# Attention over 64 heads: exponentials on VectorE assembled by addition, eight groups instead of six, four pairs transposed by DMA

## The chip, the cores and the metric

The kernel runs on one core of a Trainium2 chip. The metric is device time in microseconds of that core, as the median of several executions; the profile is of one further look at a single execution. Engines in the text: PE (TensorE: matrix products and transposes), ACT (ScalarE: exponentials), DVE (VectorE), POOL (GpSimd), SP (SyncE, which issues nearly all transfers).

## What is computed

Plain attention for 8 batches of 8 heads, 512 positions, 64 columns, all in fp32:

```python
scale = 1.0 / np.sqrt(q.shape[-1])
scores = np.einsum('bhqd,bhkd->bhqk', q, k) * scale
scores = scores - scores.max(axis=-1, keepdims=True)
attn = np.exp(scores)
attn = attn / attn.sum(axis=-1, keepdims=True)
return np.einsum('bhqk,bhkd->bhqd', attn, v)
```

The kernel leaves out the subtraction of the maximum (the inputs are normal deviates, so the scores are small) and divides at the end.

## The kernel before

**Tiling.** Two heads make a pair `g`, 32 pairs in all. For a pair, SP loads k, q and v (256 KB each, fp32, 128 partitions). POOL casts k and q to fp16 into one tile `qkp` (two casts, `cast_qk`, L334) and v into one of twelve `vp` tiles beside a column of ones (`cast_v`, L329). PE transposes `qkp` in eight 128x128 blocks into a PSUM bank `tp` (`transposes`, L351), and DVE copies the bank to `tqk` in SBUF (`copy`, L359). Scores come out transposed: a block (g, c, h) is 128 keys of chunk c against the 512 queries of head h. Two blocks make a group, one `st` tile of 128x1024 fp32 in PSUM, of which there are three; so PE can be at most three groups ahead of whoever reads them. There are 127 full groups and two halves at the end. An exponential turns `st` into `pt` in fp16 (`scores`, L368), on ACT (L388) or on DVE. A unit of `values` (L462) is four products of 128 queries: the weights are 128x128 pieces of `pt`, one from each chunk, the moving operand is `vp` with its ones column (65 columns). Seven units share a PSUM bank `o`; `normalise` (L446) takes the reciprocal of the ones columns (L449) and multiplies (L450) into a ring of 56 units, from which SP stores one head at a time (L458). `tp` and `o` share two PSUM banks, so a bank is free only when DVE has copied or normalised it.

**The exponential on DVE.** Before, a group takes seven DVE instructions. `raise_` (L399) reads the scores once from PSUM and writes z, the exponent in fixed point, as an integer whose bits are laid out as an fp32 number: this frees `st`. Six passes follow in SBUF (`pass_`, L411): m (mantissa bits with the exponent of 1.0), e (the exponent bits), and four steps of a polynomial, `scalar_tensor_tensor` with two tensor inputs (L437); the last one multiplies by e and writes fp16 into `pt`.

**The order of the work** is written out ahead by a small planner (`Plan`, L17). It steps through an imagined time, holds costs for each kind of step (L31 to L38), and decides what PE and DVE do next. Each engine then runs its list in that order and waits on semaphores where data or buffers are not there. What matters here:
- `for_dve` (L85) gives a group to DVE if the number of passes still to do is at most `AHEAD`, fewer than `MOST` were given, and the pair isn't among the last `LAST_PAIRS`.
- `step_dve` (L199) prefers a raise, then the oldest job that is due; otherwise it starts a pass, but only if every known copy or norm comes due later than the pass's end less `LATE_COPY` or `LATE_NORM`. The pass's end is its cost times `MARGIN`.
- The `values` that need a group from DVE may be planned from its last pass's end plus `SLACK` (L226).
- `step_pe` (L176) prefers scores, holds PE back for them up to `SOON`, and then takes transposes or values.

**Feeding.** `feed(g)` (L346) stands in front of the first scores of pair g. It puts the loads of pair g+5 on SP's queue and the casts of pairs g+3 (k, q) and g+2 (v) on POOL's. SP issues in order, and a load waits until POOL has cast what was in its buffer.

**The start.** `first_pair` (L521) handles pair 0 by hand. While its first loads are under way, PE runs filler products `busy` on constants (L573 to L576): six of 512 columns and two of 128.

Of the kernel before, what the change touches and what calls it, by code (L numbers as in the profile page):

```python
# [8 lines left out]
FP32 = mybir.dt.float32  # L9
# [7 lines left out]
class Plan:  # L17
# [11 lines left out]


    SLOT, EXP, EXP_DONE, EXP_FIXED = 216, 853, 181, 64  # L31
    INTO, OUT_OF = 95, 105
# [4 lines left out]
    NORM_COLUMN, PASS_DONE = 67, 80  # L37
    PASSES = (690, 950, 1335, 1335, 1335, 1250)  # L38
    FIRST_EXP = 5260
    STEP = 5  # L40
    FIRST_UNIT = 4

    LATE_NORM, LATE_COPY, HURRY, SOON, BACKLOG = 200, 200, 900, 220, 1000
    LAST_PAIRS, AHEAD, MARGIN, SLACK, MOST = 2, 0, 1.1, 2000, 6

    def __init__(self, groups, pairs, first):
        self.groups, self.pairs = groups, pairs
        self.pe, self.act, self.dve = 7000, self.FIRST_EXP, 7000
        self.m, self.tiled = first, True
        self.read = []  # L50
        self.exps = {}
        for m in range(first):
            self.act += self.EXP + self.EXP_FIXED
            self.exps[m] = self.act + self.EXP_DONE
            self.read.append(self.exps[m])
        self.tq = {0: 5800}
        self.next_t = 1
        self.part_t = 0
        self.banks = [5100, 5800]
        self.todo = [(g, h) for g in range(pairs) for h in range(2)]  # L60
        self.head = None
        self.units = self.FIRST_UNIT
        self.member = {b: m for m, grp in enumerate(groups) for b in grp}
        self.ready = []
        self.passes = []
        self.on_dve = []
        self.steps = []
# [108 lines left out]
    def step_pe(self, t):  # L176
        if self.m == len(self.groups):
            self.values(t)
            return
        g = self.groups[self.m][0][0]  # L180
        backlog = self.act - t
# [60 lines left out]
def kernel(  # L242
# [28 lines left out]
    cpool = ctx.enter_context(tc.tile_pool(name="const", bufs=1))  # L271
    lpool = ctx.enter_context(tc.tile_pool(name="load", bufs=6))
    qpool = ctx.enter_context(tc.tile_pool(name="qk16", bufs=3))
    tpool = ctx.enter_context(tc.tile_pool(name="tqk", bufs=4))
    ppool = ctx.enter_context(tc.tile_pool(name="pt", bufs=30))
    dpool = ctx.enter_context(tc.tile_pool(name="pd", bufs=3))
    wpool = ctx.enter_context(tc.tile_pool(name="work", bufs=1))
    opool = ctx.enter_context(tc.tile_pool(name="out", bufs=4))
# [4 lines left out]

    HALVED = range(20, 25)
    NU = 56
# [20 lines left out]
    def load_tile(g, name):  # L306
# [4 lines left out]
            name=f"{name}32_{g}",  # L311
            bufs=6,
        )
# [20 lines left out]
    def cast_qk(g):  # L334
# [9 lines left out]
        qkp[g] = t  # L344

    def feed(g):  # L346
        load(g + 5, "kqv")
        cast_qk(g + 3)
        cast_v(g + 2)
# [18 lines left out]
    def scores(m, on_dve):  # L368
        grp = groups[m]
        size = len(grp)  # L370
        st = ps_st.tile([P, 2, S], FP32, tag="st", name=f"st_{m}")
        pool, tag = (dpool, "pd") if on_dve else (ppool, "pt")
        pt = pool.tile([P, 2, S], FP16, tag=tag, name=f"pt_{m}")
        for x, (g, c, h) in enumerate(grp):
# [10 lines left out]
        if on_dve:  # L385
            raised[m] = {"st": st, "pt": pt}
            return
# [7 lines left out]

    QUARTIC = (-0.15702577, 12.31057107, 23.05394928, 37.67975386)
    SHIFT = -6 - 0.20724975786214195

    def raise_(m):  # L399
# [4 lines left out]
            in0=r["st"][:, :, :],  # L404
            scalar1=scale * 1.4426950408889634 * 2.0**23,
            scalar2=(127 + SHIFT) * 2.0**23,
            op0=AluOp.mult,
# [3 lines left out]
    def pass_(m, s):  # L411
        r = raised[m]
        if s == 0:
            r["m"] = wpool.tile([P, 2, S], U32, tag="m", name=f"m_{m}")
            nc.vector.tensor_scalar(  # L415
                out=r["m"][:, :, :],
                in0=r["z"][:, :, :],
                scalar1=0x007FFFFF,
                scalar2=0x3F800000,
                op0=AluOp.bitwise_and,  # L420
                op1=AluOp.bitwise_or,
            )
            return
        if s == 1:
            r["e"] = wpool.tile([P, 2, S], U32, tag="e", name=f"e_{m}")
            nc.vector.tensor_scalar(  # L426
                out=r["e"][:, :, :],
                in0=r["z"][:, :, :],
                scalar1=0xFF800000,
                scalar2=None,  # L430
                op0=AluOp.bitwise_and,
            )
            r["y"] = wpool.tile([P, 2, S], FP32, tag="y", name=f"y_{m}")
            return
        n = s - 2
        mant = r["m"][:, :, :].bitcast(FP32)
        nc.vector.scalar_tensor_tensor(  # L437
            out=r["pt"][:, :, :] if n == 3 else r["y"][:, :, :],
            in0=mant if n == 0 else r["y"][:, :, :],
            scalar=QUARTIC[n],  # L440
            in1=r["e"][:, :, :].bitcast(FP32) if n == 3 else mant,
            op0=AluOp.add,
            op1=AluOp.mult,
        )
# [76 lines left out]
    def first_pair():  # L521
# [50 lines left out]

        for n in range(6):  # L573
            busy(st0[:, 0], S)
        for n in range(2):
# [34 lines left out]
    with tc.manual_schedule():  # L610
        first_loads()
        load(1, "kq")
        load(0, "v")
        for g in range(2, 5):
            load(g, "kq")
            load(g - 1, "v")
        load(4, "v")
        make_identity(nc, ident)
# [50 lines left out]
```

## Time and profile before

Five runs: median 123.02 us, 122.82 to 123.41.

| quantity | value |
|---|---|
| profiled execution, its time | 122.82 us |
| its span (first to last instruction) | 121.0 us |
| exponentials on ACT / on DVE | 118 full groups, 2 halves and 4 of the first pair / 6 |
| DVE busy | 98.9 us, 171 instructions |
| POOL busy | 76.3 us, 93 casts on POOL after the first pair |
| PE products for scores / values / transposes | 248 / 1008 / 248, without the first and last pieces |
| DMA | 33.8 MB, mean 279 GB/s over the span |

How to read it: a group of instructions is named by its line, engine, operation and tiles (written <- read); then come its busy time, the mean duration of one, and the engine's idle time just before it with what ended that. Instructions of one engine can overlap at their ends, so count times mean is more than the busy time. A timeline row is start, length, engine, line, operation, and the idle time before it in brackets.

### The profile page before, as it was taken

To read this page: it belongs to the slowest core of one execution; us is meant where nothing else is said; L and a number is where in the kernel's file an instruction comes from. 1 tells how busy PE (TensorE), PEld (TensorE's weight loads), DVE (VectorE), ACT (ScalarE), POOL (GpSimd) and SP (SyncE) were. 2 spreads that over 40 slices of the span, in tenths; PEclk is the share of its full clock that TensorE was granted. 3 is DMA by queue.
4 is the path that set the end of the run, shared out by engine and by line. 5 is a ranking of instruction groups with operands and counts; after the bars stand their busy time and mean duration, and the time that the engine had idled before them with its cause. 6 is when DMAs were issued, how large, how long until landed. Compare 5 with 4: busy or idle time off the path is not lost.

```text
span 121.0 us, 3953 instructions
## 1 busy us (share of the span) xinstructions
PE 102.9 (85%) x1557; PEld 65.5 (54%) x1557; DVE 98.9 (82%) x171; ACT 114.4 (94%) x127; POOL 76.3 (63%) x101
## 2 busy tenths in 40 slices
PE   7977879879898899878888889987989987898970
PEld 2634455538366567544656646645655754576450
DVE  1549699999996989999999998889997999746261
ACT  4699999999999999999999999999999999999970
POOL 2368999997687968868595886268965539100000
PEclk9999999999999999999999999999999999999999
DMA  4999999997999999999969998999997994033253
GB/s 123 281 365 384 384 378 384 376 301 250 286 304 366 380 339 289 298 374 355 350 204 248 330 350 281 252 333 335 344 336 252 293 328 144 0 121 102 93 167 96
DMA packets 35604, 33.82 MB, mean 279 GB/s; under 512 B 2689, under 2 KB 35585, under 8 KB 35585
## 3 DMA queue, kind: packets, MB, share of 16 engines
q1 hardware_dynamic: 35152, 33.24, 84.6%
q10 hardware_dynamic: 432, 0.33, 0.8%
q8 instruction: 12, 0.20, 0.6%
q14 instruction: 8, 0.06, 0.2%
HBM read 25.17 MB, written 8.39 MB: 277 GB/s over the span
## 4 chain that ended last, share of the span: by engine, by line
ACT 45%; issue 19%; PE 12%; DVE 10%; DMA 4%; SPq 3%; POOL 2%; ACTq 0%; POOLq 0%
ACT pt L388 45%; PE st L383 6%; DMA q<-in_q_dram 4%; PE o L471 4%; DVE y L437 3%; SPq L327 3%; DVE tqk L364 2%; DVE ring L450 2%; PE tp L357 2%; POOL qkp L340 2%; DVE pt L437 1%; SPq L515 1%; POOL vp L332 1%; DVE rc L449 0%; DVE obl L499 0%
## 5 line engine op out<-in xcount | busy, mean ns | idle before, releaser
L388 ACT ACTIVATE pt<-st 128x1024 f16<-128x1024 f32 (+1 forms) x120 | 109.5, 1273 | 0.2
L383 PE MATMUL st<-tqk 64*128 64x512 f16 x248 | 45.5, 382 | 9.8 <-ACT pt L388 7.6
L471 PE MATMUL o<-vp,pt 128*128 128x65 f16 x1008 | 41.8, 194 | 0.7 <-POOL vp L332 0.5
L471 PEld LDWEIGHTS <-pt 128*128 128x128 f16 x1008 | 35.8, 98 | 11.8 <-issue 11.4
L340 POOL CAST qkp<-k 128x512 f16<-128x512 f32 x31 | 24.7, 795 | 21.8 <-DMA k<-in_k_dram 13.1
L332 POOL CAST vp<-v 128x512 f16<-128x512 f32 x32 | 26.9, 842 | 1.0 <-DMA v<-in_v_dram 0.8
L383 PEld LDWEIGHTS <-tqk 64*128 64x128 f16 x248 | 12.8, 93 | 25.8 <-issue 18.7
L340 POOL CAST qkp<-q 128x512 f16<-128x512 f32 x30 | 26.1, 869 | 1.1 <-DMA v<-in_v_dram 0.7
L364 DVE COPY tqk<-tp 128x1024 f16<-128x1024 f16 x30 | 20.6, 688 | 6.1 <-PE tp L357 5.3
L450 DVE TENSOR_TENSOR ring<-o,rc 128x448 f32<-128x448 f32 (+2 forms) x37 | 22.6, 612 | 1.3
L357 PE MATMUL tp<-ident,qkp 128*128 128x128 f16 x248 | 19.6, 220 | 2.8 <-DVE ring L450 1.8
L357 PEld LDWEIGHTS <-qkp 128*128 128x128 f16 x248 | 14.1, 97 | 10.4 <-POOL qkp L340 4.6
L437 DVE SCALAR_TENSOR_TENSOR y<-y,m 128x1024 f32<-128x1024 f32 x12 | 17.0, 1416 | 0.0
L449 DVE RECIPROCAL rc<-o 128x7 f32<-128x7 f32 (+2 forms) x37 | 7.3, 198 | 5.8 <-PE o L471 5.4
L437 DVE SCALAR_TENSOR_TENSOR pt<-y,e 128x1024 f16<-128x1024 f32 x6 | 8.3, 1386 | 0.1
L437 DVE SCALAR_TENSOR_TENSOR y<-m 128x1024 f32<-128x1024 f32 x6 | 8.2, 1369 | 0.0
L402 DVE TENSOR_SCALAR z<-st 128x1024 uint32<-128x1024 f32 x6 | 7.3, 1220 | 0.9 <-PE st L383 0.9
L426 DVE TENSOR_SCALAR e<-z 128x1024 uint32<-128x1024 uint32 x6 | 4.6, 771 | 0.0
L415 DVE TENSOR_SCALAR m<-z 128x1024 uint32<-128x1024 uint32 x6 | 4.4, 738 | 0.0
L519 PE MATMUL st_0a<-const-bfloat16-1.0 128*128 128x512 bf16 (+1 forms) x11 | 3.4, 480 | 0.8 <-PEq L653 0.8
L519 PEld LDWEIGHTS <-const-bfloat16-1.0 128*128 128x128 bf16 x15 | 1.7, 131 | 2.4 <-issue 2.4
L535 ACT ACT_TABLE_LOAD x1 | 1.3, 1283 | 1.7 <-PEq L653 1.7
(43 smaller groups left out, 17.8 us busy)
## 6 DMA issues: line engine op xcount, KB each, us to landing
out_dram<-ring SPq DMA_DIRECT2D x63, 128.0 KB, 3.8
k<-in_k_dram SPq DMA_DIRECT2D x31, 256.0 KB, 4.7
q<-in_q_dram SPq DMA_DIRECT2D x31, 256.0 KB, 4.8
v<-in_v_dram SPq DMA_DIRECT2D x27, 256.0 KB, 5.2
v<-in_v_dram SPq DMA_DIRECT2D x10, 128.0 KB, 4.2
k<-in_k_dram ACTq DMA_DIRECT2D x2, 128.0 KB, 2.8
q<-in_q_dram SPq DMA_DIRECT2D x2, 128.0 KB, 2.6
out_dram<-obl SPq DMA_DIRECT2D x1, 64.0 KB, 1.6
```

Source lines behind the costliest of these rows:

```text
L332: nc.gpsimd.tensor_copy(out=vps[g % NV][:, :, :, 0:D], in_=raw[g]["v"][:, :, :, :])
L340: eng.tensor_copy(out=t[:, n].rearrange("p i (h d) -> p h i d", h=2), in_=raw[g][name][:, :, :, :],)
L357: nc.tensor.transpose(tps[g][:, n, i, :], qkp[g][:, n, i, :], ident)
L364: nc.vector.tensor_copy(out=tqk[g][:, :, :], in_=tps.pop(g).rearrange("p n i c -> p n (i c)"))
L383: nc.tensor.matmul(st[:, x, :], kc, qc, start=True, stop=True)
L388: nc.scalar.activation(out=pt[:, 0:size, :], in_=st[:, 0:size, :], func=EXP, scale=scale)
L402: nc.vector.tensor_scalar(out=r["z"][:, :, :], in0=r["st"][:, :, :], scalar1=scale * 1.4426950408889634 * 2.0**23, scalar2=(127 + SHIFT) * ...
L437: nc.vector.scalar_tensor_tensor(out=r["pt"][:, :, :] if n == 3 else r["y"][:, :, :], in0=mant if n == 0 else r["y"][:, :, :], scalar=QUAR ...
L449: nc.vector.reciprocal(out=rc[:, 0:n], in_=o[:, x : x + n, D : D + 1])
L450: nc.vector.tensor_tensor(out=ring[:, u % NU : u % NU + n, :], in0=o[:, x : x + n, 0:D], in1=rc[:, 0:n].broadcast_to([P, n, D]), op=AluOp. ...
L471: nc.tensor.matmul(os[u // 7][:, u % 7, :], blocks[(g, c, h)][:, y * P : (y + 1) * P], vps[g % NV][:, h, c, :], start=(c == 0), stop=(c == ...
L519: nc.tensor.matmul(dst[:, 0:n], ones[:, 0:P], ones[:, 0:n], start=True, stop=True)
```

## The change

- **DVE's exponential.** z is now in steps of 2^-26 with the bias of fp16, so that the upper 16 bits of the integer are the bits of an fp16 number. The e pass is dropped: five passes instead of six. m becomes an integer, the polynomial's factors are scaled to it, and the last pass adds z to the polynomial and writes a 32-bit integer. Its upper half is the fp16 value; `pt` for such a group is a view of every second 16-bit word, which PE reads as weights. The work tiles z, m and y have two buffers each.
- **The planner.** `MOST` is 8 instead of 6, `AHEAD` 1 instead of 0, `MARGIN` 1.05 instead of 1.1, `SLACK` 400 instead of 2000, `LATE_NORM` and `LATE_COPY` 1300 and 1400 instead of 200, `SOON` 80 instead of 220. The groups that go to DVE are 6, 15, 29, 44, 61, 75, 88, 103; before they were 6, 23, 41, 59, 78, 97.
- **Four pairs by DMA.** `qkp` of pairs 19, 22, 25 and 28 is transposed by a DMA that SP issues in `feed`, five pairs ahead; for these pairs PE's eight transposes and DVE's copy fall away.
- **Deeper buffers.** Eight load buffers for each of k, q, v instead of six, six `qkp` instead of three, seven `tqk` instead of four. Loads run seven pairs ahead; after pairs 8, 10 and 12 those of k and q and their casts run one pair further each time. v of pairs 18 to 26 is loaded in two halves (before, 20 to 24).
- **The first filler.** 40 products of 64 columns instead of six of 512; the two of 128 stay.

```diff
-    PASSES = (690, 950, 1335, 1335, 1335, 1250)
+    PASSES = (690, 1335, 1335, 1335, 1335)
...
-    LATE_NORM, LATE_COPY, HURRY, SOON, BACKLOG = 200, 200, 900, 220, 1000
-    LAST_PAIRS, AHEAD, MARGIN, SLACK, MOST = 2, 0, 1.1, 2000, 6
+    BY_DMA = (19, 22, 25, 28)
+    LATE_NORM, LATE_COPY, HURRY, SOON, BACKLOG = 1300, 1400, 900, 80, 1000
+    LAST_PAIRS, AHEAD, MARGIN, SLACK, MOST = 2, 1, 1.05, 400, 8
...
-        self.tq = {0: 5800}
+        self.tq = {0: 5800, **{g: 0 for g in self.BY_DMA}}
...
+        while self.part_t == 0 and self.next_t in self.BY_DMA:
+            self.next_t += 1
...
-    lpool = ctx.enter_context(tc.tile_pool(name="load", bufs=6))
-    qpool = ctx.enter_context(tc.tile_pool(name="qk16", bufs=3))
-    tpool = ctx.enter_context(tc.tile_pool(name="tqk", bufs=4))
+    lpool = ctx.enter_context(tc.tile_pool(name="load", bufs=8))
+    qpool = ctx.enter_context(tc.tile_pool(name="qk16", bufs=6))
+    tpool = ctx.enter_context(tc.tile_pool(name="tqk", bufs=7))
...
-    wpool = ctx.enter_context(tc.tile_pool(name="work", bufs=1))
+    wpool = ctx.enter_context(tc.tile_pool(name="work", bufs=2))
...
-    HALVED = range(20, 25)
+    HALVED = range(18, 27)
+    SOONER = (8, 10, 12)
...
+    def transpose_by_dma(g):
+        if g not in Plan.BY_DMA:
+            return
+        tqk[g] = tpool.tile([P, 2, S], FP16, tag="tqk", name=f"tqk_{g}")
+        nc.sync.dma_start_transpose(
+            out=tqk[g].rearrange("p n (i c) -> p (n i) c", c=P),
+            in_=qkp[g].rearrange("p n i c -> p (n i c)"),
+        )
+
     def feed(g):
-        load(g + 5, "kqv")
-        cast_qk(g + 3)
+        transpose_by_dma(g + 5)
+
+        for n in range(sum(x < g for x in SOONER), sum(x <= g for x in SOONER) + 1):
+            load(g + 7 + n, "kq")
+            cast_qk(g + 3 + n)
+        load(g + 7, "v")
         cast_v(g + 2)
...
-        pool, tag = (dpool, "pd") if on_dve else (ppool, "pt")
-        pt = pool.tile([P, 2, S], FP16, tag=tag, name=f"pt_{m}")
+        if on_dve:
+            bits = dpool.tile([P, 2, S], U32, tag="pd", name=f"pd_{m}")
+            pt = bits.bitcast(FP16).rearrange("p x (s n) -> p x s n", n=2)[:, :, :, 1]
+        else:
+            pt = ppool.tile([P, 2, S], FP16, tag="pt", name=f"pt_{m}")
...
-            scalar1=scale * 1.4426950408889634 * 2.0**23,
-            scalar2=(127 + SHIFT) * 2.0**23,
+            scalar1=scale * 1.4426950408889634 * 2.0**26,
+            scalar2=15 * 2.0**26,
...
-                scalar1=0x007FFFFF,
-                scalar2=0x3F800000,
+                scalar1=0x03FFFFFF,
+                scalar2=0x04000000,
...
-        n = s - 2
-        mant = r["m"][:, :, :].bitcast(FP32)
+        n = s - 1
         nc.vector.scalar_tensor_tensor(
-            out=r["pt"][:, :, :] if n == 3 else r["y"][:, :, :],
-            in0=mant if n == 0 else r["y"][:, :, :],
+            out=r["bits"][:, :, :] if n == 3 else r["y"][:, :, :],
+            in0=r["m"][:, :, :] if n == 0 else r["y"][:, :, :],
             scalar=QUARTIC[n],
-            in1=r["e"][:, :, :].bitcast(FP32) if n == 3 else mant,
-            op0=AluOp.add,
-            op1=AluOp.mult,
+            in1=r["z"][:, :, :] if n == 3 else r["m"][:, :, :],
+            op0=AluOp.mult if n == 0 else AluOp.add,
+            op1=AluOp.add if n == 3 else AluOp.mult,
         )
...
-        for n in range(6):
-            busy(st0[:, 0], S)
+        for n in range(40):
+            busy(st0[:, 0], 64)
...
-        for g in range(2, 5):
+        for g in range(2, 7):
             load(g, "kq")
             load(g - 1, "v")
-        load(4, "v")
+        load(6, "v")
```

## The prediction

> **What bounds the kernel now.** I read the profile from the outside in: the busy shares, the timeline of the busiest engine, the costliest groups, then the busy time in stretches and the timeline of the engine that the change loads.
>
> ```profile
> span 121.0 us, 3953 instructions
> PE 102.9 (85%) x1557; PEld 65.5 (54%) x1557; DVE 98.9 (82%) x171; ACT 114.4 (94%) x127; POOL 76.3 (63%) x101
> ```
>
> ScalarE (ACT) leads with 94%. Its own timeline says how it is spent:
>
> ```profile
> 7.65 109.65 ACT L388 ACTIVATE pt<-st 128x1024 f16<-128x1024 f32 x120
> ```
>
> From 7.65 us to 117.30 us ACT runs one exponential after another as a single merged piece. The span ends 3.7 us later. So ACT sets the time, and VectorE (DVE), which takes 6 of the groups off it, is the only relief.
>
> ```profile
> L388 ACT ACTIVATE pt<-st 128x1024 f16<-128x1024 f32 (+1 forms) x120 | 109.5, 1273 | 0.2
> ...
> L364 DVE COPY tqk<-tp 128x1024 f16<-128x1024 f16 x30 | 20.6, 688 | 6.1 <-PE tp L357 5.3
> ...
> L437 DVE SCALAR_TENSOR_TENSOR y<-y,m 128x1024 f32<-128x1024 f32 x12 | 17.0, 1416 | 0.0
> ...
> L437 DVE SCALAR_TENSOR_TENSOR pt<-y,e 128x1024 f16<-128x1024 f32 x6 | 8.3, 1386 | 0.1
> L437 DVE SCALAR_TENSOR_TENSOR y<-m 128x1024 f32<-128x1024 f32 x6 | 8.2, 1369 | 0.0
> L402 DVE TENSOR_SCALAR z<-st 128x1024 uint32<-128x1024 f32 x6 | 7.3, 1220 | 0.9 <-PE st L383 0.9
> ...
> ```
>
> The mean of 1273 ns for one exponential overlaps its neighbours; the busy time is the price. 120 instructions hold 118 full groups and two halves, so one full group costs 109.5 / 119 = 0.92 us of ACT. The rows of L437, L402 and the two bit operations price an exponential on DVE:
>
> ```profile
> L426 DVE TENSOR_SCALAR e<-z 128x1024 uint32<-128x1024 uint32 x6 | 4.6, 771 | 0.0
> L415 DVE TENSOR_SCALAR m<-z 128x1024 uint32<-128x1024 uint32 x6 | 4.4, 738 | 0.0
> ```
>
> How much room DVE has is in the busy times by stretch (columns: stretch, length, then busy us and count of PE, PEld, DVE, ACT, POOL, the clock, DMA):
>
> ```profile
> 9.00:110.00 101.00, 88.25 (x1374) 56.79 (x1372) 91.04 (x137) 100.93 (x111) 72.54 (x90) 1.00 0.93 300
> ...
> 54.00:70.00 16.00, 14.08 (x230) 9.19 (x229) 15.13 (x23) 16.00 (x18) 11.85 (x15) 1.00 0.94 302
> ```
>
> From the first raise to the last copy (9 to 110 us) DVE is busy 91.0 of 101.0 us: 10.0 us are free. In the densest stretch it idles 0.87 of 16 us, 5.4%.
>
> **Part 1: two more groups on DVE.** ACT loses two full groups: 2 x 0.92 = -1.84 us. Nothing else on ACT changes, so this is the most that the change can bring.
>
> **Part 2: what DVE pays.** Durations in DVE's timeline overlap the next instruction a little:
>
> ```profile
> 58.69 0.69 DVE L364 COPY tqk<-tp 128x1024 f16<-128x1024 f16 x1 [0.17 <-PE tp L357]
> ...
> 67.41 1.22 DVE L437 SCALAR_TENSOR_TENSOR y<-y,m 128x1024 f32<-128x1024 f32 x1
> 68.54 0.20 DVE L449 RECIPROCAL rc<-o 128x7 f32<-128x7 f32 x1
> ```
>
> The pass at 67.41 lasts 1.22 us and the next starts after 1.13, the copy at 58.69 is followed after 0.61 (59.30); I take 0.08 off each instruction. A group now: z 1.22, m 0.74, e 0.77, y 1.37 + 1.42 + 1.42, last 1.39 = 8.33, less 7 x 0.08 = 7.77 us. The new group has no e pass, and the last pass adds z itself: 7.56 - 6 x 0.08 = 7.08 us. The four two-input passes keep their shape and size (1024 elements, 32 bits in); that integer inputs or a 32-bit result cost nothing extra is read from z, which already writes 32-bit integers, and from y<-y,m, which already writes 32 bits at 1416 against 1386 ns for 16 bits. So DVE's exponentials go from 6 x 7.77 = 46.6 to 8 x 7.08 = 56.6: +10.0 us. The transposes by DMA take away four copies of 0.69 - 0.08: -2.4 us. Net +7.6: the same stretch holds 91.0 + 7.6 = 98.6 us of DVE work. To let ACT have its whole 1.84 us, DVE would have to do this in 101.0 - 1.84 = 99.2 us, 0.6% idle.
>
> What idle is left to it no row shows directly. Bounds: 0.6% at one end (then the gain is -1.84), 5.4%, the densest stretch of the table, at the other: 98.6 / 0.946 = 104.2 us, +3.2. Between them stands the run from 57.06 to 69.39 in the timeline, where the only idle is the 0.17 us before the copy at 58.69: 1.4% of 12.3 us. I take that one, because it is the row with the most passes back to back, and the new rules (a pass may now start though a copy or a norm comes due up to 1.3 us before its end; z, m and y have two buffers; a second group may be raised with one pass left) make such runs the normal case. 98.6 / 0.986 = 100.0 us, 1.0 less than now. So of the 1.84 us DVE gives back 0.84, in exponentials that start late because a raise, a copy or a norm stands behind a pass. The cover for those delays is the three score buffers, about two exponentials (1.8 us) ahead; a pass of 1.4 us just fits, two do not.
>
> **Part 3: contention of DVE and GpSimd (POOL).**
>
> ```profile
> 66.41 0.61 POOL L332 CAST vp<-v 128x512 f16<-128x512 f32 x1
> 67.55 1.54 POOL L340 CAST qkp<-k 128x512 f16<-128x512 f32 x1 [0.53 <-DMA k<-in_k_dram]
> ```
>
> The cast that began beside the pass at 67.41 took 1.54 us, the one before it 0.61, and L437's own passes range from 1215 to 1604 ns. So the two engines hold each other up. POOL's casts average 795 to 869 ns, some 0.22 over 0.61, for 93 of them 21 us, or 0.87 per pass of L437; eight more passes add 7.0 us to the 72.5 busy in the stretch, 79.5 of 100. That is covered by POOL's free time and by the deeper buffers (8 loads, 6 casts, 7 transposed pairs), and I cost it at nothing; without that cover, a late cast delays its transposes and scores one for one. On DVE, if all 32 passes took the longest time seen (1604 against a mean of 1.40) it would be 32 x 0.20 = +6.5 us; below, 32 x (1.40 - 1.215) = -5.9. I keep the present mean, since POOL's amount of work stays.
>
> The Trainium skill speaks against the change here: "SBUF — State Buffer", section Who interferes with whom, says that a VectorE instruction with two SBUF inputs and a GpSimd instruction reading SBUF exclude each other on one port for the whole instruction. The trace agrees in kind (0.61 against 1.54 us). By the rule, added up with starts 1.13 us apart for 32 passes, 0.56 for about 92 casts and 0.60 for 8 m passes, the port would be taken 92.5 of some 100 us, and a sum made by it would give the whole gain away to waiting.
>
> **Part 4: transposes by DMA (pairs 19, 22, 25, 28).** PE loses 4 x 8 transposes (in the chain, eight take 0.55 us): -2.2 us, off the path. SP gets four issues, each waiting for POOL's casts of that pair; behind it stand the loads of pair g+7 and the stores. The nearest row for a transfer of this size is
>
> ```profile
> k<-in_k_dram SPq DMA_DIRECT2D x31, 256.0 KB, 4.7
> ```
>
> The transpose is issued five pairs ahead; in DVE's timeline five copies of pairs span 50.44 to 66.03 us, so the cover is 15.6 us less the casts' lateness. From below it costs what a load does (hidden); from above I have only the cover: what a transfer takes beyond some 15 us stalls PE and then ACT, four times. I take nothing. The loads behind it run seven pairs ahead (over 20 us), the stores have a ring of 14 heads.
>
> The Trainium skill, "VectorE: DVE Perf Modes", section The three transpose paths, gives 1309 ns for one 128x128 transpose through DMA; eight in a row would be an estimated 10.5 us, still inside the cover. No run here shows one yet.
>
> **Part 5: weights read with a gap.** PE now loads 64 of 1008 weights from every second 16-bit word. Now a load and its product follow each other every 32 ns (44 of L471 take 1.58 us in PE's timeline, its last product lasting 0.19), with the load's own 98 ns hidden. Bounds: hidden again, 0; all of it exposed, 64 x (98 - 32) = 4.2 us of PE work in eight places of 0.53. PE is free 12% of the time (14.08 of 16), 0.44 us a pair, so 0.1 would be left eight times: +0.7 us. A gain is excluded, since nothing gets shorter. I take 0, the row being the same instruction at the same size.
>
> **Part 6: the first filler.**
>
> ```profile
> 0.78 2.93 PE L519 MATMUL st_0a<-const-bfloat16-1.0 128*128 128x512 bf16 x8 [0.78 <-PEq L653]
> ...
> 3.13 0.29 DVE L533 CAST q<-q 128x256 f16<-128x256 f32 x1 [1.84 <-DMA q<-in_q_dram]
> ...
> 3.50 0.42 PE L557 MATMUL tp_qa<-ident,q 128*128 128x128 f16 x2
> ```
>
> The first transpose starts at 3.50, when the cast (3.42) has just ended and the filler too: 3072 + 256 columns in 2.72 us, 0.82 ns each. 40 x 64 + 256 = 2816 columns end at 0.78 + 2.30 = 3.08, before the cast, so the start stays: 0. If instead each short product cost as much as its weight load (131 ns in the group's row, against 52), it would end 40 x 0.079 = 3.2 later, at 6.2: +2.7 at most. From below only the 0.02 us between cast and start are to be had. I take 0, by the columns.
>
> **The sum.** Profiled execution 122.82 us (span 121.0 and 1.8 around it): -1.84 + 0.84 + 0 + 0 + 0 + 0 = -1.0, so 121.8. The median of the runs is 0.2 above the profiled one: **122.0 us**.
>
> **The rivals.**
> - *ACT alone decides.* DVE keeps up with 0.6% idle: 123.02 - 1.84 = 121.2. For: DVE idles on PE now (5.4 + 5.3 us of waits), and PE gets freer. Against: passes are not divisible. 10%.
> - *DVE eats the gain.* At 2.4% idle its work fills the old 101 us: 123.0. For: nothing but a row of 12 us carries my 1.4%. 13%.
> - *DVE becomes the bound, slower.* Place: between 9 and 110 us; price: the present density of 5.4% gives +3.2, 126.2; halfway, 3.5%, gives 102.2 and 124.2. It decides as soon as DVE idles over 2.4%, or if the passes lengthen by more than 1.0 us in all, 0.03 each, through POOL. 12%.
> - *A transfer or the filler is late* (Parts 4 and 6, or the change doing less than it says because PE waits for a transposed pair): +0.5 to +2.7 against the forecast, 122.5 to 124.7. 5%.
>
> **How the numbers follow.** The forecast has 60%; its own range, from 1% to 2% idle, is 121.6 to 122.6. The likeliest time is 122.0. A measurement of this kernel tells about 0.3% (0.37 us) from no change. Faster: 60 + 10 = 70%; the same: 13%, the second rival; slower: 12 + 5 = 17%. The range reaches from 121.1 (the first rival) into the slower cases to 123.5; outside are most of the third and fourth, about 15%.
>
> **What would show it.** Right: L388 with 118 instructions and about 107.7 us busy; DVE busy near 106 us and 98 to 99% in the long stretch; ACT's timeline in a few pieces with about 0.8 us of gaps, each ended by PE, and PE before it by DVE's z, tqk or ring. Wrong: L437's mean above 1.45 us (contention), PE waiting on a tqk written by DMA, L471's spacing above 32 ns, the first exponential after 4.87 us. If ACT still is one piece and L388 holds 120 x 0.92 us, the step that removed groups from ACT is what failed.

## The result, and the profile after

| | before | after |
|---|---|---|
| median of the runs | 123.16 us (87 runs) | 123.95 us (45 runs, 122.23 to 127.86) |
| ratio to the kernel before | 1 | 1.0006, 95% interval 0.9994 to 1.0019 |
| profiled execution / its span | 122.82 / 121.0 us | 123.95 / 122.2 us |

Every ratio here counts only runs within 1.5% of their kernel's fastest, which leaves out 21 of the changed kernel's 45 (13 took over 125 us) but none of `e1`'s, so that ratios of kernels with different scatter are not quite alike. By the ratio the change brought nothing, by the median it costs 0.6%, and the scatter is wider. 122.0 was forecast. The page of the changed kernel (engines' busy time, then the granted clock in 40 slices):

```profile
span 122.2 us, 3956 instructions
...
PE 103.6 (85%) x1559; PEld 66.2 (54%) x1559; DVE 104.6 (86%) x173; ACT 112.8 (92%) x125; POOL 79.0 (65%) x101
...
PEclk9999999999999999999999999998599999999999
```

ACT has 1.6 us less to do than before, yet the span is 1.2 longer. The 5 in the clock's row is new: before, the row held nothing of the kind. The groups that were added or moved:

```profile
L409 ACT ACTIVATE pt<-st 128x1024 f16<-128x1024 f32 (+1 forms) x118 | 107.8, 1192 | 1.9 <-PE st L404 1.9
...
L482 PEld LDWEIGHTS <-pt 128*128 128x128 f16 x944 | 36.0, 99 | 11.3 <-issue 7.3
L345 POOL CAST qkp<-k 128x512 f16<-128x512 f32 x31 | 25.5, 822 | 16.1 <-DMA tqk<-qkp 11.6
...
L448 DVE SCALAR_TENSOR_TENSOR y<-y,m 128x1024 f32<-128x1024 f32 x16 | 22.2, 1389 | 0.0
...
L382 DVE COPY tqk<-tp 128x1024 f16<-128x1024 f16 x26 | 17.7, 680 | 0.0
...
L448 DVE SCALAR_TENSOR_TENSOR pd<-y,z 128x1024 uint32<-128x1024 f32 x8 | 10.8, 1347 | 0.0
L424 DVE TENSOR_SCALAR z<-st 128x1024 uint32<-128x1024 f32 x8 | 9.7, 1216 | 0.9 <-PE st L404 0.9
```

ACT lost exactly its two groups (118 instructions, 107.8 us), and the passes cost what was forecast (1347 to 1407 ns). The cast row holds a new wait: POOL stood 11.6 us for the DMA that reads `qkp`. ACT's timeline (start, length, and in brackets the idle time before) shows where its gain went:

```profile
8.81 1.02 ACT L409 ACTIVATE pt<-st 128x1024 f16<-128x1024 f32 x1
10.52 35.88 ACT L409 ACTIVATE pt<-st 128x1024 f16<-128x1024 f32 x39 [0.69 <-PE st L404]
46.72 40.44 ACT L409 ACTIVATE pt<-st 128x1024 f16<-128x1024 f32 x44 [0.32 <-PE st L404]
88.00 30.42 ACT L409 ACTIVATE pt<-st 128x1024 f16<-128x1024 f32 x34 [0.84 <-PE st L404]
```

One piece has become four. Counted from the end of one exponential to the end of the next, less the 0.917 us of a full one, the holes after the fourth exponential are 2.20 us, against 0.37 before; the three largest are 0.79 at 10.52, 0.43 at 46.72 and 0.95 at 88.00. The books for the end of the last exponential, 117.30 before and 118.42 after: -1.84 for the two groups, +1.12 at the start (the fourth exponential ends at 8.91 instead of 7.79), +1.83 more holes: +1.1. What follows it is as long as before (3.7 us).

The hole at 88.00 can be followed back. Busy times by stretch (columns as in the prediction), in steps of the clock's own 3.41 us:

```profile
77.92:81.33 3.41, 3.35 (x54) 2.08 (x51) 3.00 (x4) 3.41 (x6) 2.34 (x3) 1.00 1.11 358
81.33:84.75 3.42, 1.85 (x10) 0.49 (x9) 3.39 (x6) 3.42 (x5) 3.42 (x5) 1.00 0.94 324
84.75:88.16 3.41, 3.41 (x42) 2.55 (x40) 2.58 (x4) 2.57 (x4) 2.29 (x3) 0.50 0.97 308
```

From 81.33 to 84.75 PE was busy for 1.85 of 3.42 us (54%); in the next stretch its clock is 0.50, it works without a break, and ACT runs dry. Why PE had so little to do is in the timelines of POOL, DVE and PE:

```profile
78.99 0.61 POOL L345 CAST qkp<-k 128x512 f16<-128x512 f32 x1 [5.47 <-DMA tqk<-qkp]
79.55 1.60 POOL L345 CAST qkp<-q 128x512 f16<-128x512 f32 x1
...
79.04 3.18 DVE L448 SCALAR_TENSOR_TENSOR y<-y,m 128x1024 f32<-128x1024 f32 x2
82.15 1.21 DVE L424 TENSOR_SCALAR z<-st 128x1024 uint32<-128x1024 f32 x1
83.28 0.67 DVE L382 COPY tqk<-tp 128x1024 f16<-128x1024 f16 x1
...
80.20 0.62 PE L375 MATMUL tp<-ident,qkp 128*128 128x128 f16 x8
80.66 0.29 PE L482 MATMUL o<-vp,pt 128*128 128x65 f16 x4
80.88 0.39 PE L404 MATMUL st<-tqk 64*128 64x512 f16 x2
81.71 0.39 PE L404 MATMUL st<-tqk 64*128 64x512 f16 x2 [0.44 <-ACT pt L409]
82.63 0.39 PE L404 MATMUL st<-tqk 64*128 64x512 f16 x2 [0.52 <-ACT pt L409]
83.41 0.39 PE L404 MATMUL st<-tqk 64*128 64x512 f16 x2 [0.39 <-DVE z L424]
```

The transposes of 80.20 were done at 80.82, but their copy came at 83.28, behind the second of two passes (1.6 us each, beside casts of 1.60) and a z. The other shared bank waited for its normalise, which began at 83.88. So both banks were taken, and PE's list had scores alone there. POOL, released only at 78.99, ran its late casts just then.

The other two holes aren't behind a pass of DVE. Ahead of 10.52 PE was still slow: eight transposes of pair 1 took 1.04 us from 8.20 on, before the full clock of 9.65, against 0.68 us from 6.84 on in the kernel before. That hole belongs to the start. Ahead of 46.72 PE's list had 28 products of `values` (44.91 to 45.98) in front of the scores that ACT waited for.

### The profile page after: what moved, and what is told of

It reads as the page before. It is cut to its first block, busy times and chain, and to the rows that moved or that the text cites. A ratio compares the mean times of both kernels' runs of the same rounds, so it can differ in the third digit from the quotient of the medians.

```text
span 122.2 us, 3956 instructions
## 1 busy us (share of the span) xinstructions
PE 103.6 (85%) x1559; PEld 66.2 (54%) x1559; DVE 104.6 (86%) x173; ACT 112.8 (92%) x125; POOL 79.0 (65%) x101
## 4 chain that ended last, share of the span: by engine, by line
ACT 36%; PE 26%; DVE 25%; issue 8%; DMA 2%; ACTq 0%
ACT pt L409 36%; PE st L404 11%; PE o L482 9%; DVE y L448 8%; DVE tqk L382 5%; DVE ring L461 4%; PE tp L375 3%; DVE z L424 3%; DMA q<-in_q_dram 2%; DVE pd L448 2%; DVE m L438 1%; DVE rc L460 1%; PE st L573 1%; DVE tqk L380 1%; PE tp_qb L568 0%
## 5 line engine op out<-in xcount | busy, mean ns | idle before, releaser
L409 ACT ACTIVATE pt<-st 128x1024 f16<-128x1024 f32 (+1 forms) x118 | 107.8, 1192 | 1.9 <-PE st L404 1.9
L345 POOL CAST qkp<-k 128x512 f16<-128x512 f32 x31 | 25.5, 822 | 16.1 <-DMA tqk<-qkp 11.6
L345 POOL CAST qkp<-q 128x512 f16<-128x512 f32 x30 | 32.1, 1068 | 0.7 <-DMA q<-in_q_dram 0.5
L337 POOL CAST vp<-v 128x512 f16<-128x512 f32 x32 | 23.4, 735 | 7.1 <-DMA v<-in_v_dram 7.0
L448 DVE SCALAR_TENSOR_TENSOR y<-y,m 128x1024 f32<-128x1024 f32 x16 | 22.2, 1389 | 0.0
L382 DVE COPY tqk<-tp 128x1024 f16<-128x1024 f16 x26 | 17.7, 680 | 0.0
L448 DVE SCALAR_TENSOR_TENSOR y<-m 128x1024 f32<-128x1024 uint32 x8 | 11.3, 1407 | 0.2
L448 DVE SCALAR_TENSOR_TENSOR pd<-y,z 128x1024 uint32<-128x1024 f32 x8 | 10.8, 1347 | 0.0
L424 DVE TENSOR_SCALAR z<-st 128x1024 uint32<-128x1024 f32 x8 | 9.7, 1216 | 0.9 <-PE st L404 0.9
L482 PE MATMUL o<-vp,pd 128*128 128x65 f16 x64 | 9.5, 195 | 0.6 <-DVE pd L448 0.5
L482 PEld LDWEIGHTS <-pd 128*128 128x128 f16 x64 | 6.3, 98 | 1.9 <-issue 0.9
L530 PE MATMUL st_0a<-const-bfloat16-1.0 128*128 128x64 bf16 (+1 forms) x45 | 3.0, 248 | 0.8 <-PEq L664 0.8
```

The lines of the kernel that those rows point to most:

```text
L337: nc.gpsimd.tensor_copy(out=vps[g % NV][:, :, :, 0:D], in_=raw[g]["v"][:, :, :, :])
L345: eng.tensor_copy(out=t[:, n].rearrange("p i (h d) -> p h i d", h=2), in_=raw[g][name][:, :, :, :],)
L382: nc.vector.tensor_copy(out=tqk[g][:, :, :], in_=tps.pop(g).rearrange("p n i c -> p n (i c)"))
L409: nc.scalar.activation(out=pt[:, 0:size, :], in_=st[:, 0:size, :], func=EXP, scale=scale)
L424: nc.vector.tensor_scalar(out=r["z"][:, :, :], in0=r["st"][:, :, :], scalar1=scale * 1.4426950408889634 * 2.0**26, scalar2=15 * 2.0**26, o ...
L448: nc.vector.scalar_tensor_tensor(out=r["bits"][:, :, :] if n == 3 else r["y"][:, :, :], in0=r["m"][:, :, :] if n == 0 else r["y"][:, :, :] ...
```

## The experiments

Four theories of what opens the holes. **C**: PE's clock, late in full at the start and halved where PE has too little work. **D**: DVE's passes, too dense and beside POOL's casts. **S**: the DMA transposes, late themselves and holding up SP and POOL. **F** (from e9 on): the deeper feeding costs by itself. All but `e12` were timed beside the kernel before, and the ratios are to it.

### The start and the density (C, D, S)

`e1`, the long filler back; `e2`, beside it a filler ahead of the scores of eight late pairs; `e3`, the long filler and no pairs by DMA; `e4`, the kernel before with the short filler alone. The long filler (`e1`, `e2`, `e3`), then the pairs (`e3`):

```diff
-        for n in range(40):
-            busy(st0[:, 0], 64)
+        for n in range(6):
+            busy(st0[:, 0], S)
```
```diff
-    BY_DMA = (19, 22, 25, 28)
+    BY_DMA = ()
```

> The changed kernel with the first filler of before (six products of 512 columns). Theory C (PE loses its full clock in two places: at the start, because the short filler ends 0.8 us before the first transposes, and later where a pair is transposed by DMA and PE has too little to do): the full clock from about 4.5 us instead of 9.65, the first exponential at 4.9 to 5.3 us instead of 5.4 and no gaps of 0.6 and 0.8 us behind it, the median of the runs about 1.2 us below the changed kernel's 123.95, still spread over 2 us or more because of the later place. Rival D (DVE and POOL hold each other up, and DVE is the bound): the median stays within 0.4 us of 123.95.

> As e1, and in addition three filler products of 128 columns in front of each group of scores of the pairs 18, 19, 21, 22, 24, 25, 27 and 28 (written into the score tile before the scores overwrite it, some 0.16 us of PE a group). Theory C: no half-clock stretch in the middle, the spread of the runs shrinks to about that of the kernel before (1 us), median 121.8 to 122.4. Rival D: PE only gets more to do, so the time is that of e1 or up to 0.5 us longer and the spread stays. Rival S (the DMA transposes hold up SP and POOL): spread and median as in e1.

> As e1, but no pair is transposed by DMA: PE transposes all and DVE copies all 31 (four more copies, +2.4 us of DVE work in a stretch that has 4.3 us free). Theory C: the spread shrinks to about 1 us, no half-clock stretch, the median 122.5 to 124.5 by DVE's extra work. Rival D: wide spread stays, and the median rises by the whole 2.4 us over e1. Rival S: like theory C, so this run alone does not tell C from S; e2 does.

> The kernel before with the short first filler (40 products of 64 columns) and nothing else. Theory C: the start alone costs, so the lowest time stays near 122.7, the median rises by 0.5 to 1.5 us, and the spread grows from 1 us to 2 or more, with the full clock coming after 4.5 us in the profile. Rivals D and S: no change, 123.1.

Measured: e1 123.77 us, ratio 1.0051 (1.0027 to 1.0075); e2 125.67, 1.0234; e3 124.28, 1.0092 (1.0071 to 1.0113); e4 123.15, 1.0004 (0.9987 to 1.0020). In the kernel before, the short filler alone costs nothing that can be measured. With the long one in the changed kernel the record of the full clock begins at 4.3 us instead of 9.7, the fourth exponential ends 0.93 earlier and the last one 1.08 earlier (117.34), although a hole of 1.06 us opens at 16.8 us. Yet the median falls by only 0.2. In `e1`'s profile the program ended 4.1 us after it had issued its last store, against 2.7 in the changed kernel's; why isn't seen. So what the late start costs the median stays open between 0.2 and 1.1 us. Over all profiles the fourth exponential ends at 8.53 with the short filler (mean of 8) and at 8.00 with the long one (12). e2 shows that PE has no room for extra products: ACT's holes grew to 6 us. Without the pairs by DMA (e3) the median is 0.5 above e1's; DVE has four copies more, 2.4 us, but that these are the cause isn't shown.

### One part alone

`e5`: the kernel before with only the new exponential, six groups. `e6`: the same with `MOST = 7` (groups 6, 22, 37, 53, 69, 86, 102). `e7`: only the feeding, the buffers and the pairs by DMA. `e8`: the changed kernel with `MOST = 6`. (`e7` keeps the old exponential, rules and filler.)

> The kernel before with only the new exponential (five passes, 32-bit result, weights read with a gap), still six groups on DVE, the old planner rules, feeding and filler. ACT's work is the same 118 full groups, DVE has 6 x 0.69 = 4.1 us less. C (PE's clock is lost where PE has too little work or a hole at the start): PE's work is untouched, so no half-clock stretch after the start, 122.8 to 123.3. D (DVE's passes, dense and beside POOL's casts, make the bubbles): less DVE work, 0.0 to 0.3 less than before, 122.8 to 123.2. If the new passes themselves were slower or the weights with a gap cost PE something: above 123.5.

> As the one with only the new exponential, but a seventh group on DVE (groups 6, 22, 37, 53, 69, 86, 102) under the old planner rules. ACT loses one full group, -0.92 us; DVE has 7 x 7.08 = 49.6 instead of 46.6 us of exponentials, +3.0. C: PE keeps all transposes and the old start, no half-clock stretch: 122.1 to 122.5. D: the old rules leave DVE 7 us of idle in the long stretch, few bubbles: 122.1 to 122.7. If DVE's amount of work alone decides, half of the gain is given back: 122.6 to 123.2.

> The kernel before with only the new feeding, buffers and the four pairs by DMA; the old exponential, six groups, old planner rules, old filler. ACT's work is unchanged, DVE has 2.4 us less of copies. C: PE has four pairs without transposes, so half-clock stretches come up between 80 and 100 us: mean clock below 0.985 in at least a third of the runs, median 123.3 to 124.5. D: DVE has less to do and no denser passes: 122.9 to 123.3, clock as before. S (the DMA transposes hold up SP and POOL): bubbles of ACT behind late casts or loads after 60 us, 123.5 to 125.

> The changed kernel with six groups on DVE instead of eight (6, 15, 29, 44, 61, 75), all else as changed. ACT gets two full groups back, +1.84 us; DVE loses 14.2 us of work, all of it after 87 us. C: the short filler's late start (0.5 to 1.4 us) and the half-clock stretches remain, so +1.8 over the changed kernel less what DVE's late bubbles cost: 124.8 to 125.8. D: the bubbles before 75 us stay, those after go: 124.0 to 125.0. If eight groups were what makes DVE the bound, six give the time before: 123.0 to 123.5.

Measured: e5 123.40, 1.0014 (0.9985 to 1.0043); e6 122.93, 0.9969 (0.9936 to 1.0002); e7 124.17, 1.0070 (1.0041 to 1.0098); e8 126.12, 1.0122 (1.0064 to 1.0180). ACT's timeline of e6:

```profile
7.96 108.53 ACT L391 ACTIVATE pt<-st 128x1024 f16<-128x1024 f32 x119
```

It is one piece, as in the kernel before, and ends at 116.49 instead of 117.30: of the 0.92 us of the seventh group 0.81 are gained. The runs show less, 0.28 us in the median, with an interval that just reaches 1. So the exponential itself does no harm. The feeding with the pairs by DMA loses 1.0 us with the old exponential, six groups and the old rules: that is not D. e8 has the highest median of the timed kernels, 2.2 us above the changed kernel's. ACT's two groups more explain 1.84 of that, but DVE has 13 us less to do (91.6 us busy), and nothing of it comes back: this speaks against D too. Why e8 is so slow isn't seen: its profile is of one of its two short runs.

### Eight groups, the feeding, and a second profile

`e9`: new exponential and new planner rules, eight groups, two work buffers; old feeding, old filler, no pairs by DMA. `e10`: only the new feeding and buffers, no pairs by DMA. `e11`: as e9 with milder rules (the edit below). `e12`: the changed kernel once more.

```diff
-    LATE_NORM, LATE_COPY, HURRY, SOON, BACKLOG = 1300, 1400, 900, 80, 1000
+    LATE_NORM, LATE_COPY, HURRY, SOON, BACKLOG = 500, 500, 900, 220, 1000
```

> The new exponential with the new planner rules and two buffers for z, m, y: eight groups on DVE (6, 15, 29, 44, 61, 75, 88, 103) as in the changed kernel; but the old feeding and buffers, no pairs by DMA, the old long filler. F (new theory: the new feeding alone costs some 0.7 to 0.9, whatever the exponential does): -1.84 with few bubbles, 121.6 to 122.4. D (dense passes of eight groups make the bubbles): ACT's bubbles at 46 us and between 14 and 40 us stay, 0.8 or more in all, 122.6 to 124. C has little to lose here, since PE keeps all transposes: no half-clock stretch after the start.

> The kernel before with only the new feeding and buffers, no pairs by DMA; the old exponential, six groups, old rules and filler. Beside the one with the four pairs by DMA (124.17). F: the deeper loads cost by themselves, 123.6 to 124.2. S (the DMA transposes hold up SP and POOL): 122.9 to 123.4, the pairs by DMA are the cost. C: no half-clock stretch in either case, 123.0 to 123.4 and a smaller spread than with the pairs by DMA.

> As the one with the new exponential, eight groups and old feeding, but under milder rules: late copies and norms up to 0.5 us instead of 1.3 and 1.4, PE held back for scores up to 220 instead of 80; groups 6, 16, 33, 46, 65, 81, 97, 114. D: a copy or a norm behind a pass is what opens bubbles, so this one keeps more of the gain than the new rules do, 121.3 to 122.3, and by 0.3 or more the better of the two. F: both the same within 0.3, 121.5 to 122.4. If the number of groups alone decides (DVE full), both lose alike, above 122.6.

> The changed kernel once more, for a second profile. C: the place of the half-clock stretches follows PE's activity, so again one after a place where PE has only scores to do (between 60 and 100 us, pairs without transposes) and a late full clock at the start; time 122.7 without, 124.0 with one, 125.3 with two. If the first profile's stretch at 84.75 us was an accident, none or one elsewhere.

Measured: e9 124.01, 1.0077 (1.0050 to 1.0103); e10 123.70, 1.0031 (1.0011 to 1.0051); e11 124.03, 1.0108 (1.0065 to 1.0150); e12 127.3, a single run. In e9 ACT's timeline breaks at DVE:

```profile
19.82 25.88 ACT L391 ACTIVATE pt<-st 128x1024 f16<-128x1024 f32 x28 [0.23 <-PE st L386]
45.94 28.52 ACT L391 ACTIVATE pt<-st 128x1024 f16<-128x1024 f32 x31 [0.24 <-PE st L386]
75.28 42.49 ACT L391 ACTIVATE pt<-st 128x1024 f16<-128x1024 f32 x47 [0.82 <-PE st L386]
```

and ahead of the last break DVE and PE stood so:

```profile
72.92 1.22 DVE L428 SCALAR_TENSOR_TENSOR pd<-y,z 128x1024 uint32<-128x1024 f32 x1
74.05 1.28 DVE L364 COPY tqk<-tp 128x1024 f16<-128x1024 f16 x2
...
73.15 0.61 PE L357 MATMUL tp<-ident,qkp 128*128 128x128 f16 x8 [0.26 <-DVE ring L441]
74.79 0.82 PE L386 MATMUL st<-tqk 64*128 64x512 f16 x6 [1.04 <-DVE tqk L364]
```

A copy waits behind one pass, both banks hold transposes, and PE waits 1.04 us for `tqk`. The holes are 2.13 us in all, though the clock was full from 6.7 us on, and 0.93 of them are this one: here D is shown, without the feeding, the DMA and the short filler. The hole at 45.94 (0.35) has 28 products of `values` in front of the scores, as in the changed kernel. ACT's last exponential ended at 117.77, later than the 117.30 before, although ACT had two groups less. In e11 the milder rules left 0.17 us of holes, and ACT's last exponential ended at 115.85. DVE was less dense there too (5.7% idle from 9 to 110 us, 3.3% in e9), so rules and density aren't told apart. And they put the eighth group at 114, so that pair 28's values come after pair 31's, an order that the closing lines aren't written for: only the time up to 115.85 is read, not the total.

The feeding alone (e10) costs 0.3%, so in the medians e7's pairs by DMA add 0.5 us to it. In e10's profile pair 1's k lands a microsecond later than before, and ACT has one hole, 1.18 us, at 9.7 us. e12 shows S at its plainest. PE's timeline, then the stretches:

```profile
80.95 0.29 PE L482 MATMUL o<-vp,pt 128*128 128x65 f16 x4
83.73 0.82 PE L404 MATMUL st<-tqk 64*128 64x512 f16 x6 [2.49 <-DMA tqk<-qkp]
```
```profile
81.33:84.75 3.42, 0.82 (x6) 0.30 (x7) 1.07 (x2) 1.85 (x3) 0.95 (x2) 1.00 1.11 356
84.75:88.16 3.41, 2.72 (x20) 1.48 (x20) 3.38 (x5) 3.41 (x5) 3.41 (x6) 0.50 0.94 313
88.16:91.57 3.41, 3.41 (x50) 2.48 (x48) 2.16 (x5) 2.31 (x4) 1.72 (x3) 0.50 0.97 292
```

Pair 22's transpose, issued by SP at 76.57, landed at 83.69; its scores were due at 81.2. PE waits 2.49 us and then runs at half clock for two stretches; ACT's holes add up to 5.7 us. A third such stretch follows at 101.82. The first is at the same place as in the first profile, 84.75, as C expected.

### Taking single waits away

`e13`: eight `qkp` buffers (28 `pt`). `e14`: `LATE_COPY = 200` alone. `e15`: milder rules and the long filler on the changed kernel (groups up to 109). `e16`: both, e15 and eight `qkp`. The edit of `e13` to `qkp`:

```diff
-    qpool = ctx.enter_context(tc.tile_pool(name="qk16", bufs=6))
+    qpool = ctx.enter_context(tc.tile_pool(name="qk16", bufs=8))
```

> The changed kernel with eight qkp buffers instead of six (and 28 pt buffers instead of 30, to make room). S: POOL's three waits for the DMA transposes (11.6 us in all) shrink to under 3 us, casts come earlier, the runs scatter less; median 122.6 to 123.3. D: the waits shrink, but the holes behind DVE's passes stay; 123.6 to 124.3 and runs up to 127 as before. C: as D, unless PE is fed in the stretch from 81.3 to 84.8 us, where it was busy 0.54 of the time.

> The changed kernel with only LATE_COPY back at 200 instead of 1400: no pass starts if a copy of a transposed pair comes due before its end. Eight groups still (6, 15, 30, 46, 62, 75, 91, 107). D: the holes at 46 us and near 87 us go, -0.8 to -1.4: 122.5 to 123.2. S: POOL's waits are the cause, no change: 123.6 to 124.3. C: if PE no longer idles for a copy while both banks are full, no half-clock stretch in the middle; the late full clock at the start stays, about 1.

> The changed kernel with milder rules (copies and norms at most 0.5 us behind a pass, PE held back up to 220 for scores) and the long filler of the kernel before; the feeding and the four pairs by DMA stay; groups 6, 16, 33, 46, 65, 79, 93, 109. D and C: full clock from 5 us, holes in ACT under 0.6 us after the start, last exponential near 116: 121.7 to 122.6, better than both kernels. S: POOL's waits and late transposes still cost, 122.8 to 124 with a wide scatter. F (the deeper feeding costs 0.5 by itself): 122.2 to 123.0.

> The same with eight qkp buffers (28 pt). S: POOL's waits go, so 0.5 to 1.2 better than the one with six, 121.6 to 122.6. D and C: the same as the one with six within 0.3.

Measured: e13 123.28, 0.9985 (0.9955 to 1.0015), 122.21 to 126.90; e14 124.25, 1.0041 (1.0008 to 1.0073); e15 125.83, 1.0082 (1.0041 to 1.0123); e16 124.64, 1.0092 (1.0059 to 1.0126). With two more buffers the median is 0.7 us lower, which a scatter of 4.7 us doesn't make certain, and POOL's waits for the transposes are gone from the profile. That profile, of a run of 122.72 us, has eight groups under the new rules, DVE 3.9% idle from 9 to 110 us, and only 1.03 us of holes: density alone doesn't open them. D's remedies fail here: with copies ahead of passes (e14) the hole near 87 us goes, but 2.35 us remain in all (1.12 at 10.0, 0.43 at 34.7 and at 48), and e15 is slower than the changed kernel. Its profile fell on an execution of 129.62 us, with the same event as e12, at pair 25 instead of 22:

```profile
90.39 0.19 PE L482 MATMUL o<-vp,pd 128*128 128x65 f16 x1
93.72 0.61 PE L404 MATMUL st<-tqk 64*128 64x512 f16 x2 [3.14 <-DMA tqk<-qkp]
```

### Fewer loads ahead of the transposes

SP issues in order. Measured from the first scores of the pair in whose `feed` a load stands, SP issued v's loads 0 to 5 us later before the change and 9 to 15 us later, from pair 12 on, after it. The transposes stand in the same queue. `e17` takes the loads back to five pairs ahead, `e18` does so with eight `qkp`. The edit of both to the loads:

```diff
-            load(g + 7 + n, "kq")
+            load(g + 5 + n, "kq")
...
-        load(g + 7, "v")
+        load(g + 5, "v")
...
-        for g in range(2, 7):
+        for g in range(2, 5):
...
-        load(6, "v")
+        load(4, "v")
```

> The changed kernel with loads only five pairs ahead as before (three more for k and q after pairs 8, 10 and 12, as the casts need), eight load buffers kept, five pairs loaded at the start. S (SP's queue is behind by the loads asked for earlier, and the transposes with it): SP's lag behind the scores falls from 10 to 15 us to 4 to 9, the transposes land 6 us or more before their scores, the runs no longer reach above 125.5, median 122.5 to 123.3. D or C alone: lag and scatter don't matter or stay, 123.6 to 124.3.

> The same with eight qkp buffers and 28 pt buffers, so that POOL doesn't stop for a transpose either. S: 122.0 to 122.9 and a narrow scatter, better than the changed kernel by over 1 and than the kernel before. D: the holes of DVE's passes remain and eat the gain, 123.0 to 124. C: the late full clock at the start alone costs some 1, 122.8 to 123.5.

Measured: e17 123.56, 1.0024 (0.9996 to 1.0052), all 12 runs between 122.63 and 123.99; e18 122.73, 0.9936 (0.9904 to 0.9968), but from 121.75 to 127.44. The half-clock stretch in e17's profile is at 15.85 us, in e15's the first is at 20.6, where no pair goes by DMA. How long before its pair's first scores each transpose had landed, from the traces:

| us ahead, pair | 19 | 22 | 25 | 28 |
|---|---|---|---|---|
| after, first profile | 5.1 | 2.0 | 2.4 | 2.3 |
| after, second (e12) | 2.5 | 0.05, PE waited | 0.05, PE waited | 2.0 |
| e15 | 4.0 | 0.3 | 0.05, PE waited | 2.2 |
| e17 | 8.2 | 5.9 | 5.3 | 4.0 |
| e18 | 6.6 | 4.3 | 0.05, PE waited | 2.8 |

In e17 the lag fell to 6 to 12 us, the transposes gained 2 to 4, and no run was long; its median missed the 122.5 to 123.3 that S expected, with a mean clock near 0.985 in most runs. In e18 the lag was up to 15 again though the loads stand where they do in e17, and three of its runs took over 125. So the loads asked for earlier aren't the only thing that holds SP back; what else does isn't settled. e18 is the best of all, 0.6% below the kernel before by the ratio and 0.2% by the median.

Two counts over all runs: of the kernels with pairs by DMA (e2 and e12 left out) 37 of 137 runs took over 125 us, though none of the 12 of e1 and of the 12 of e17; of e3, e4, e5, e6, e9, e10 and e11, which have none, 4 of 66, two of them e11's. The runs are from several chips. On the two on which both kinds ran in number it is 7 of 18 against 1 of 24 (e5 to e8) and 14 of 38 against 2 of 24 (e9 to e16).

## Why the prediction was wrong, step by step

- **Part 1 was right**: -1.84 us of ACT, 118 exponentials in 107.8 us; in e6's profile 0.81 of one such step is kept.
- **Part 2, "1.4% idle", so 0.84 given back**, is the first term that failed. The work was sized somewhat too high (DVE's busy time grew by 5.7 us, forecast 7.6). The idle time was sized far too low: the row of 12 us was misread, because the brackets of a timeline leave out short idle times, and seven gaps, six of them of 0.03 to 0.04 us, add up there. By busy time (here DVE's alone, then the clock and DMA), the measure of the two bounds, that row before the change and the long stretch after it are

```profile
57.06:69.39 12.33, 11.95 (x20) 1.00 0.90 283
```
```profile
9.00:110.00 101.00, 88.02 (x1339) 55.59 (x1337) 96.66 (x139) 99.15 (x109) 75.47 (x90) 0.98 0.99 309
```

So the row itself had 0.38 us idle, 3.1%, and with it the forecast's own sum is 98.6 / 0.969 = 101.8, 0.8 longer than before instead of 1.0 shorter: 123.8. After the change DVE was busy 96.66 of 101.0 us, 4.3% idle, so that it filled the old stretch; the least idle of any profile was 2.5% (e3). In e9, where nothing but exponential, rules and groups changed, 2.13 us of holes stood instead of 0.84, and the kernel was slower than before; only in e13's profile are they near it, 1.03. The claim that three score buffers cover one pass missed the other resource: two PSUM banks shared by transposes and values. A copy behind a pass keeps one taken, and PE then has scores alone.
- **Part 4, the DMA transposes at nothing**, failed in both halves. The transfer is quick (3.7 to 7.1 us from issue to landing, with the queue in it; by the Trainium skill's "VectorE: DVE Perf Modes", section The three transpose paths, eight blocks one after another were an estimated 10.5), but the cover wasn't 15.6 us less the casts' lateness: casts were done 8 to 14 us before SP came to the issue in the changed kernel's two profiles. What was left was 0 to 5 us. And a transpose holds its `qkp` buffer, which stopped POOL for up to 5.5 us at a time, a wait that the step didn't name; e13, without it, is 0.7 us lower in the median, within its scatter. That PE loses 2.2 us of transposes "off the path" was true and perhaps not harmless: in both profiles of the changed kernel PE's busy share fell to 54% or less in pair 22. Stretches nearly as empty or emptier stand in e15 and e17 at 12 to 21 us too, where PE keeps its transposes.
- **Part 6, "the start stays"**: the columns were right (the filler ended before the cast), but the filler ended at 3.28 and PE stood idle 0.6 us before its first real product at 3.87 (q also landed 0.4 later), and the full clock came at 9.7 instead of 4.4 us. In the profile +1.12 us stand there, and the hole at 10.52 (0.79) comes on top: in that one execution the start is the largest miss of all. In the median of e1 only 0.2 of it comes back, so its share of the 0.8 between the medians is open.
- **Part 3, contention at nothing**: the mean passes stayed (1389 ns against 1416), as said. But single passes and casts of 1.6 us side by side are in the chain to the hole at 88.00. Its share wasn't measured by itself. The rule of the Trainium skill that was weighed there ("SBUF — State Buffer", section Who interferes with whom) would have given the whole gain to waiting. The gain is gone, but banks, start, queue and clock have their parts in that, so the runs neither prove nor refute its sum.
- **Part 5 was right**: the weights of `pd`, read with a gap, load in 98 ns, against the 99 of `pt`.

The rivals: the ratio (1.0006) is nearest to "DVE eats the gain", 123.0 us; the median, 123.95, is nearest to the halfway case of "DVE becomes the bound, slower", 124.2. That the row read rightly gives 123.8 is luck in part: DVE's work came out smaller, and the start and the transposes, both put at nothing, moved too. The long runs go with the pairs by DMA: that follows from the counts and from the two traces of long runs, in which PE waited 2.5 and 3.1 us for such a transfer (e12, e15). That every long run had one was not seen, and a wait of 0.7 us at pair 25 in e13's profile went with 122.72 us. Nor are the pairs by DMA the whole excess: e9 and e3, which have none, stand at 124.01 and 124.28. How the 0.8 us divides among rules, start, feeding and transposes isn't settled.

## What to carry to other kernels

Cover for a transfer is counted on the queue that issues it: take from the profile when that queue reaches the instruction, not when its data are ready. Idle shares that are to be compared are taken from busy time over each stretch, not from the waits that a timeline prints. Before an engine is loaded further, look at what it releases (here banks that two users share), because a single late copy there idles another engine. And an engine that is relieved "off the path" may still lose by it: where its clock follows its activity, too little work in one stretch can make the next one slower.

## What was not expected of the hardware

In the traces PE's clock was halved for 3.41 us, or a multiple of it, after each of eight stretches of 3.41 us at the full clock in which PE was busy 24 to 54.7% of the time; after four of 55 to 58% the full clock was kept, after one of 58% (e2) it was halved. In the first profile's stretch no single idle time of PE was longer than 0.52 us, in the eight the longest was 0.5 to 2.4 us, in the four 1.0 to 1.3. The Trainium skill, "TensorE: Matmul & The Clock Gate", section Why this matters for your kernels, asks that PE have no idle gaps over about 3 us. That was kept here, and the clock fell all the same: the busy share of the stretch tells the cases apart, the longest gap doesn't. In the changed kernel one such stretch goes with about 1.3 us: with 47 of its executions sorted by how many the mean clock amounts to, the medians were 122.75, 123.98, 125.3 and 126.7 us for none to three (11, 22, 8 and 6 executions). A 512-column product that lasts 386 ns as a mean took up to 614 in the half-clock stretch of the first profile. A DMA transpose of one pair occupied SP for 1.2 to 2.6 us, against 0.4 to 0.5 for most loads.
